# A11 of the first FFN step by products: loaded into the place of that step's own results

## The chip, the core and the metric

The kernel runs on one core of a Trainium2 chip. The core has a matrix engine (PE; its weight loads are listed as PEld), a vector engine (DVE), an activation engine (ACT), a general engine (POOL) and a queue engine (SP) that mostly issues DMA transfers. Each engine works through its own list of instructions in order; an instruction that waits holds up everything behind it on that engine. All transfers, whether SP, POOL or ACT issues them, are carried by the core's 16 DMA engines.

The metric is the device time of one execution in microseconds (us), given as the median of several runs.

## The reference

A two-layer network over 512 tokens of 1024 features: layer 0 mixes by dilated window attention, layer 1 by an mLSTM, and each is followed by a gated feed-forward part (FFN). The change lies in the first half of the FFN:

```python
def swiglu(xn, w_in, w_out):
    gu = xn @ w_in
    return (jax.nn.silu(gu[..., :D_FF]) * gu[..., D_FF:]) @ w_out
...
        h = h + swiglu(rms_norm(h, ffn_norm[i]), ffn_w_in[i], ffn_w_out[i])
```

with `D_FF` = 2816. All values are 32-bit floats.

## The kernel before

**Precision.** A product in full precision is made of three matmuls: each operand is split into a high part (rounded, made by ACT) and a low part (the rest, made by DVE), and high times high, high times low and low times high are added in PSUM (`SPLITS`). A weight tile of 128 x 1024 so costs ACT one copy (L209) and DVE one subtraction (L210) before PE can use it. The split weights live in three rotating buffers, the raw ones (`wraw`) in three as well.

**The FFN's first half** (`ffn_in`) runs over 22 blocks of 128 output columns, two at a time, j = 0, 2, ... 20. For j = 0 and 2 it works in the plain way (`plain`): PE multiplies weights by the split tokens, chunk by chunk, the result is scaled by the inverse norm (L982) and gated into a tile `hid` (L987). From j = 4 on (`PLAIN` = 4) it uses a scheme of seven products in place of eight (`PRODUCTS`): the weights of the two halves (gate and up) and of the two halves of the features form a 2 x 2 block A11, A12, A21, A22, the tokens a 2 x 2 block B11 to B22, and sums of both are multiplied.

- `normalized` makes the token operands once for each layer while the plain steps run on PE. It writes the normed tokens into two tiles, both of the rotating tag `w8` (two buffers): the first holds B11 and B12, the second B21 and B22. From these it makes T1 (L927), T3 (L932), T2 (L939) and T4 (L947), each in place or in the tile `t1`, and splits all of them (L909, L914). For B11 and T1 the low part is not a DVE subtraction: ACT writes minus the high part (L911) and a POOL transfer adds the raw values on the fly (L912).
- `weights_of(j)` loads the four weight tiles of a step (L1003, all on SP, in the order A11, A22, A12, A21). A11 and A21 lie in the two halves of a `w8` tile, that is, for j = 4 in the place of the first tokens' tile, for j = 6 in that of the second, and so on by turns; A22 and A12 lie in `wraw` buffers. `prepare` splits one operand after another, two products ahead of PE (`AHEAD`), and makes the sums (L1011): S1 = A21 + A22 and S2 = S1 - A11 in the tile `t1` (which T1 held), S3 = A11 - A21 in the place of A21, S4 = A12 - S2 in that of A12.
- `products(j)` issues the seven products in the order p1 (A11 B11), p5 (S1 T1), p6 (S2 T2), p2 (A12 B21), p7 (S3 T3), p3 (S4 B22), p4 (A22 T4), each 24 matmuls of 256 columns (L1040). The bank `u` starts as a copy of p1's result (L1052, ACT), takes p6, p7 and p4, and is read in between: after p7 by the addition into v5 (L1046, DVE). The results go into `hidden(j // 2)`: one half after p3 (L1079), one after p4 (L1083).

`hidden(i)` is a tile for each pair of blocks with its own tag and place; for i = 2, which belongs to j = 4, it is a tile of the FFN's own pool, `hid2`. Its space belongs to the mixer's tiles until the mixer is done, and is then not used until j = 4 writes its results.

Beside this, the first FFN (`output_products`) loads sums of output weight rows ahead of time: a plain load (L1161, SP) and a load that adds (L1162, POOL). The second FFN turns the residual: a DVE transpose (`hB`, L1690) and four stores on POOL (`hD`, L1693), and it loads and scales the final gains on POOL (L1711, L1712).

**What sets the order.** The program is written as above, but the framework's scheduler decides the order on each engine from estimated durations and dependences, for DMA issues on SP and POOL too. Tiles of one tag rotate: a new tile may be written when the last reader of the old one in the same bytes is done.

Of the kernel before, what the change touches and what calls it, by code (L numbers as in the profile page):

```python
# [71 lines left out]
def tile_hybrid_dilated_attn_mlstm(  # L72
# [131 lines left out]
    def split_chunk(chunk):  # L204

        raw, n, view, name = chunk
        hi = wp.tile([P, 1024], F32R, tag="whi", name=name + "_h", bufs=W_BUFS)
        lo = wp.tile([P, 1024], F32R, tag="wlo", name=name + "_l", bufs=W_BUFS)
        nc.scalar.activation(hi[:, :n], raw[:, :n], AF.Copy)  # L209
        nc.vector.tensor_tensor(lo[:, :n], raw[:, :n], hi[:, :n].bitcast(F32), op=ALU.subtract)  # L210
        return view(hi), view(lo)
# [147 lines left out]
    with ExitStack() as actx:  # L359
# [16 lines left out]
        ang, n, sn, cs = (tmp[:, 0, i * P:(i + 1) * P] for i in range(4))  # L376
# [497 lines left out]
    PLAIN = 4  # L874
    AHEAD = 2

    def ffn_in(layer, fp, pair, rbc, hook, following, hid, during):
# [11 lines left out]
        def place(i, name, dtype):  # L889
            p, tag = (xp, "x%d" % (i - 3)) if 3 <= i < 11 else (fp, "hid%d" % i)  # L890
            return p.tile([P, 2, SEQ], dtype, tag=tag, name="f%d%s%d" % (layer, name, i))

        def hidden(i):
            return place(i, "hid", F32)
# [98 lines left out]
        def weights_of(j):  # L993

            nm = "f%dj%d" % (layer, j)
            w8 = fp.tile([P, 2, 1024], F32, tag="w8", name=nm + "_w8", bufs=2)
            w = {"A11": w8[:, 0], "A21": w8[:, 1]}
            for key in ("A22", "A12"):
                w[key] = wp.tile([P, 1024], F32, tag="wraw", name=nm + key, bufs=W_BUFS)
            for key in ("A11", "A22", "A12", "A21"):  # L1000
                half, ch = int(key[1]) - 1, int(key[2]) - 1
                c0 = half * D_FF + j * P
                nc.sync.dma_start(w[key].rearrange("p (k n) -> p k n", k=4),  # L1003
                                  wi[ch * 4 * P:(ch + 1) * 4 * P, c0:c0 + 256].rearrange("(k p) n -> p k n", p=P))

            def split(key):
                return split_chunk((w[key], 1024, lambda t: t.rearrange("p (k n) -> p k n", k=4), nm + key))

            def total(key, a, b, op, place):
                w[key] = w[place]  # L1010
                nc.vector.tensor_tensor(w[key], w[a], w[b], op=op)  # L1011
            w["own"] = fp.tile([P, 1024], F32, tag="t1", name=nm + "S")
            made = {}

            def prepare(key):
                made[key] = split(key)

                if key == "A11":
                    total("S1", "A21", "A22", ALU.add, "own")
                elif key == "S1":  # L1020
                    total("S2", "S1", "A11", ALU.subtract, "own")
                elif key == "S2":
                    total("S3", "A11", "A21", ALU.subtract, "A21")
                elif key == "A12":
                    total("S4", "A12", "S2", ALU.subtract, "A12")
            return [(lambda key=key: prepare(key)) for key, _ in PRODUCTS], made
# [65 lines left out]
        def prepare(n):  # L1092
            if n < len(todo):
                j, i = todo[n]
                if j not in prepared:
                    prepared[j] = weights_of(j)
                prepared[j][0][i]()
            else:
                following(n - len(todo))
# [732 lines left out]
```

## Time and profile before

| | us |
|---|---|
| median of 3 runs | 1411.19 |
| range of the runs | 1411.02 to 1411.64 |
| the profiled execution | 1411.64 |
| its span, first to last instruction | 1409.9 |
| PE busy in the span | 1393.7 |
| DVE busy in the span | 1063.9 |

The profile is that of one execution. A row of a timeline gives the start (us from the span's start), the duration, engine, line, operation, output <- inputs with their sizes, and in brackets the idle time of the engine before it and what ended it. A row of a group ends with busy time, mean duration and idle time; a row of a tile's or line's view gives the count, the shortest, median and longest duration in ns, and the first and last start. A row of waits reads "who waited <- for whom: total us, times, longest". Names leave out buffer numbers, and a name that ends in one loses it: `f0j4A_h` is the high part of A11, A12 or A22 of layer 0's step j = 4, `f0j4S` one of its sums, `f0j_w` its `w8` tile, `f0x` a tile of normed tokens, `f0j_c`, `f0j_p` and `f0j_u` the banks c11, p5 and u. "DMA to landing" is the time from the issue of a transfer to its arrival.

### The profile page before, as it was taken

Reading aid. Unit: us, or ns where it says so; the run is one execution under the profiler, and the core shown is the slowest. Engines: PE = TensorE matmul, PEld = TensorE weight load, DVE = VectorE, ACT = ScalarE, POOL = GpSimd, SP = SyncE. Lnnn points to the kernel's source line nnn. Section 1 sums busy time; section 2 is a strip of 40 time slices with the busy share of each in tenths; the row PEclk is TensorE's granted clock in tenths of the full one; section 3 lists DMA queues with packets and bytes.
Section 4 is the critical chain, followed back from the end, with each engine's and each line's share of the span. In section 5 each row is a group of like instructions: output and inputs, shape, how many; then the busy total and the mean of one; then the engine's idle time right before and its main releaser. Section 6 shows DMA issues by size and latency. Waiting matters only on the chain. (4 is left out here: it accounts for less than half of the span.)

```text
span 1409.9 us, 21577 instructions
## 1 busy us (share of the span) xinstructions
PE 1393.7 (99%) x8370; PEld 1243.1 (88%) x8370; DVE 1063.9 (75%) x1838; ACT 677.8 (48%) x1127; POOL 153.5 (11%) x226
## 2 busy tenths in 40 slices
PE   9999999999999999999999999999999999999998
PEld 7888888888888888999999998888888899999886
DVE  7866557566567299877877898998758988887875
ACT  5333224224225254444576463786535544458744
POOL 1011011002002000000000101113101320001111
PEclk9999999999999999999999999999999999999999
DMA  6346245335434447333253733234334743335871
GB/s 194 96 114 196 82 118 160 119 106 131 159 105 121 155 145 175 115 120 114 83 171 83 162 109 105 81 87 105 101 98 116 213 123 121 120 107 118 174 193 60
DMA packets 138623, 178.15 MB, mean 126 GB/s; under 512 B 8660, under 2 KB 112404, under 8 KB 138520
## 3 DMA queue, kind: packets, MB, share of 16 engines
q1 hardware_dynamic: 121392, 134.17, 30.7%
q0 software_dynamic: 15472, 41.47, 13.4%
q8 instruction: 66, 1.08, 0.3%
q10 hardware_dynamic: 1656, 1.12, 0.2%
q14 instruction: 37, 0.30, 0.1%
HBM read 158.91 MB, written 15.73 MB: 124 GB/s over the span
## 5 line engine op out<-in xcount | busy, mean ns | idle before, releaser
L1162 POOL DMA_DIRECT2D f0S<-in_ffn_w_out_dram x10 | 8.7, 898 | 255.8 <-DVE f0hid L1079 173.6
L1187 POOL DMA_DIRECT2D f1T<-in_ffn_w_out_dram x12 | 14.3, 1189 | 197.2 <-ACT f1T L1190 169.8
L1693 POOL DMA_DIRECT2D hD<-hB x32 | 21.7, 695 | 70.2 <-DVE hB L1690 70.0
L552 DVE TENSOR_TENSOR rot<-rot,sinr 32x1024 f32<-32x1024 f32 x24 | 28.8, 1205 | 0.0
L240 PE MATMUL mo<-n_h,mo_k_h 128*128 128x512 f32 x64 | 25.3, 396 | 0.0
L240 PE MATMUL mo<-n_h,mo_k_l 128*128 128x512 f32 x64 | 25.2, 394 | 0.0
L240 PE MATMUL mwo<-yo_l,mwo_k_h 128*128 128x512 f32 x64 | 25.1, 393 | 0.0
L240 PE MATMUL mqk<-n_h,mqk_k_h 128*128 128x512 f32 x64 | 25.1, 392 | 0.0
L240 PE MATMUL mo<-n_l,mo_k_h 128*128 128x512 f32 x64 | 25.1, 392 | 0.0
L240 PE MATMUL awo<-ao_h,awo_k_h 128*128 128x512 f32 x64 | 25.1, 392 | 0.0
L240 PE MATMUL mqk<-n_l,mqk_k_h 128*128 128x512 f32 x64 | 25.1, 392 | 0.0
L240 PE MATMUL f0j<-n_h,f0j_h 128*128 128x512 f32 x64 | 25.0, 391 | 0.0
L240 PE MATMUL f1j<-n_h,f1j_h 128*128 128x512 f32 x64 | 25.0, 391 | 0.0
L240 PE MATMUL mwo<-yo_h,mwo_k_l 128*128 128x512 f32 x64 | 25.0, 391 | 0.0
L240 PE MATMUL mqk<-n_h,mqk_k_l 128*128 128x512 f32 x64 | 25.0, 391 | 0.0
L240 PE MATMUL awo<-ao_h,awo_k_l 128*128 128x512 f32 x64 | 25.0, 390 | 0.0
L240 PE MATMUL f1j<-n_h,f1j_l 128*128 128x512 f32 x64 | 25.0, 390 | 0.0
L240 PE MATMUL awo<-ao_l,awo_k_h 128*128 128x512 f32 x64 | 25.0, 390 | 0.0
L240 PE MATMUL f0j<-n_h,f0j_l 128*128 128x512 f32 x64 | 24.9, 390 | 0.0
L240 PE MATMUL f0j<-n_l,f0j_h 128*128 128x512 f32 x64 | 24.9, 389 | 0.0
L240 PE MATMUL f1j<-n_l,f1j_h 128*128 128x512 f32 x64 | 24.9, 389 | 0.0
L240 PE MATMUL mwo<-yo_h,mwo_k_h 128*128 128x512 f32 x64 | 24.8, 391 | 0.0
(2406 smaller groups left out, 5619.3 us busy)
## 6 DMA issues: line engine op xcount, KB each, us to landing
f0j_w<-in_ffn_w_in_dram SPq DMA_DIRECT2D x26, 512.0 KB, 4.9
f1j_w<-in_ffn_w_in_dram SPq DMA_DIRECT2D x26, 512.0 KB, 5.2
f1T<-in_ffn_w_out_dram POOLq DMA_DIRECT2D x12, 512.0 KB, 7.2
awo_k_w<-in_attn_w_out_dram SPq DMA_DIRECT2D x8, 512.0 KB, 7.0
mv_k_w<-in_mlstm_w_in_dram SPq DMA_DIRECT2D x8, 512.0 KB, 3.7
mqk_k_w<-in_mlstm_w_in_dram SPq DMA_DIRECT2D x8, 512.0 KB, 3.7
mo_k_w<-in_mlstm_w_in_dram SPq DMA_DIRECT2D x8, 512.0 KB, 4.1
mwo_k_w<-in_mlstm_w_out_dram SPq DMA_DIRECT2D x8, 512.0 KB, 3.5
```

The costliest lines, as they stand in the source:

```text
L240: nc.tensor.matmul(acc, whl[a][:, k, m * P:(m + 1) * P], pairs[b][kk], start=(kk == 0 and (a, b) == SPLITS[0]), stop=(kk == nk - 1 and (a, ...
L552: nc.vector.tensor_tensor(sh, sh, sinr.unsqueeze(1).to_broadcast([R, 2, SEQ]), op=ALU.mult)
L1162: nc.gpsimd.dma_start(t, src[1][:, ks], accum_op=ALU.add)
L1187: nc.gpsimd.dma_start(view(to), weight_rows(hk * UNITS + u, n), accum_op=ALU.add)
L1693: nc.gpsimd.dma_start(hD[k // 4].rearrange("(b i) x -> i b x", i=R)[:, :, c0:c0 + R], t[R * a_:R * (a_ + 1)])
```

## The change

For j = 4 alone, A11 is loaded into a tile from `hidden(2)`, the place that later takes the results of the same step, and not into the first half of the `w8` tile. A21 stays where it was.

```diff
             w8 = fp.tile([P, 2, 1024], F32, tag="w8", name=nm + "_w8", bufs=2)
-            w = {"A11": w8[:, 0], "A21": w8[:, 1]}
+
+            a11 = hidden(j // 2).rearrange("p k n -> p (k n)") if j == PLAIN else w8[:, 0]
+            w = {"A11": a11, "A21": w8[:, 1]}
             for key in ("A22", "A12"):
```

The step's own `hidden(2)` call in p3 then takes the same tag a second time; all readers of A11 (its split and the sums S2 and S3) stand ahead of p3 on their engines. The number and kinds of instructions are the same; the line numbers behind the edit grow by two. In the built program the scheduler's order differs around the start of j = 4 in both layers: the load of A11 stands further ahead on SP, and on DVE the split of A11 and the sums stand further ahead, T4 and its split further back; in layer 1 residual transposes and the loading of the final gains also change places.

## The prediction

> **What bounds the kernel now.** I read the page first, then who waits for whom on PE, then the starts of PE's products.
>
> ```profile
> span 1409.9 us, 21577 instructions
> PE 1393.7 (99%) x8370; PEld 1243.1 (88%) x8370; DVE 1063.9 (75%) x1838; ACT 677.8 (48%) x1127; POOL 153.5 (11%) x226
> ```
>
> PE is busy for 99% of the span, so only a place where it stops can give time. Three of its longer waits lie in the step the change touches:
>
> ```profile
> PE f1j_p L1040 <- DVE f1j4S_l L210: 1.3, 1, 1.3
> ...
> PE f0j_u L1040 <- ACT f0j_u L1052: 1.1, 1, 1.1
> ...
> PE f0j_u L1040 <- DVE f0j4S_l L210: 0.7, 1, 0.7
> ```
>
> The ends of matmuls are modelled, so the loss is better read from starts. The first product of a step, A11 times B11, begins (last numbers: first and last start) at:
>
> ```profile
> L1040 PE MATMUL f0j_c<-f0B11h,f0j4A_h x8: 277/283/284, 549.0 to 551.5; 128*128 128x256 f32 x8
> L1040 PE MATMUL f0j_c<-f0B11h,f0j6A_h x8: 282/283/284, 571.6 to 574.1; 128*128 128x256 f32 x8
> L1040 PE MATMUL f0j_c<-f0B11h,f0j8A_h x8: 283/283/284, 591.7 to 594.2; 128*128 128x256 f32 x8
> L1040 PE MATMUL f1j_c<-f1B11h,f1j4A_h x8: 278/283/284, 1109.1 to 1111.6; 128*128 128x256 f32 x8
> L1040 PE MATMUL f1j_c<-f1B11h,f1j6A_h x8: 283/284/284, 1132.3 to 1134.8; 128*128 128x256 f32 x8
> ```
>
> Step j=6 lasts 591.7 - 571.6 = 20.1 us: seven products of 2.87 us, without a gap. Step j=4 lasts 22.6 in layer 0 and 23.2 in layer 1. The excess, 2.5 + 3.1 = **5.6 us**, is all that the change can win in these steps. In the first of them DVE, not PE, is the full engine:
>
> ```profile
> 548.95:571.60 22.65, 20.83 (x170) 20.35 (x169) 21.20 (x24) 10.74 (x13) 2.60 (x3) 1.00 0.76 209
> ```
>
> (length; PE, PEld, DVE, ACT, POOL busy; clock; DMA share; GB/s). DVE is full because it stood still just before (timeline of DVE, and one row of ACT):
>
> ```profile
> 536.47 1.22 DVE L914 TENSOR_TENSOR f0T3l<-f0x,f0T3h 128x1024 fp32r<-128x1024 f32 x1
> ...
> 541.70 1.22 DVE L947 TENSOR_TENSOR f0x<-f0x 128x1024 f32<-128x1024 f32 x1
> ...
> 545.11 1.06 ACT L209 ACTIVATE f0j4A_h<-f0j_w 128x1024 fp32r<-128x1024 f32 x1 [5.19 <-DMA f0j_w<-in_ffn_w_in_dram]
> ...
> 546.21 1.23 DVE L210 TENSOR_TENSOR f0j4A_l<-f0j_w,f0j4A_h 128x1024 fp32r<-128x1024 f32 x1 [3.29 <-ACT f0j4A_h L209]
> ...
> 547.95 1.22 DVE L1011 TENSOR_TENSOR f0j4S<-f0j_w,f0j4A 128x1024 f32<-128x1024 f32 x1
> 549.08 1.22 DVE L914 TENSOR_TENSOR f0T4l<-f0x,f0T4h 128x1024 fp32r<-128x1024 f32 x1
> 550.22 0.69 DVE L982 TENSOR_TENSOR f0j2gu<-f0j,n1rbc 128x512 f32<-128x512 f32 x1
> ...
> 561.16 1.22 DVE L1011 TENSOR_TENSOR f0j6S<-f0j_w,f0j6A 128x1024 f32<-128x1024 f32 x1
> ...
> 566.00 0.69 DVE L1046 TENSOR_TENSOR f0j4v<-f0j_u,f0j4v 128x512 f32<-128x512 f32 x1 [0.20 <-PE f0j_u L1040]
> ```
>
> T3's low part (536.47) is the last reader of the first tokens' tile; only then may A11 be fetched into it. It lands at 545.1, DVE idles 3.29 us for its split, and S1 = A21 + A22 starts at 547.95.
>
> **The change part by part.** *Removed:* A11's wait for the tokens. Its load goes, in the built order, to a place long ahead: behind the first plain weight load of layer 0 and before the last load of the mLSTM's output weights in layer 1. In layer 0 it waits there for the last attention matmul that reads the space of `hid2`. There the DMA engines are idle:
>
> ```profile
> 485.00:490.00 5.00, 5.00 (x24) 4.14 (x23) 0.09 (x1) 0.00 (x0) 0.00 (x0) 1.00 0.00 0
> ```
>
> The next load on SP needs a weight buffer that is still in use, so I cost the early load at nothing. Were it held longer, the plain weights behind it would be late, and PE would pay each us in full.
>
> *Not removed:* A21 still goes into the tokens' tile, after T3, and S1 also overwrites T1, which the accumulating transfer of T1's low part must have read. So S1 moves up only as far as these two land sooner:
>
> ```profile
> L912 POOL DMA_DIRECT2D f0T1l<-f0t x1: 877/877/877, 537.6 to 537.6; - x1
> ...
> DMA to landing us min/median/max: 7.7/7.7/7.7
> ```
>
> ```profile
> q1 hardware_dynamic: 1556, 1.55, 59.3%
> q0 software_dynamic: 144, 0.52, 36.3%
> ```
>
> ```profile
> 546.00:548.00 2.00, 2.00 (x10) 1.68 (x9) 1.79 (x3) 1.64 (x3) 0.00 (x0) 1.00 0.00 1
> ```
>
> From 538 to 546 SP's three weight loads took 59.3% of 8 us, 1.6 us each; T1's transfer landed at 545.3, and all was quiet by 546 (A21 landed near 545.8). Without A11 the same work ends 1.6 us sooner: S1 can start at 544.3. Bounds: 543.3 if A21 and T1 share well, 545.1 if A21 gets no more than A11's old place.
>
> Layer 1, in the same way:
>
> ```profile
> L1003 SPq DMA_DIRECT2D f1j_w<-in_ffn_w_in_dram x2: 368/918/1467, 1099.5 to 1099.9; - x2
> ...
> DMA to landing us min/median/max: 7.8/7.8/7.8
> ```
>
> ```profile
> 1106.10 1.06 ACT L209 ACTIVATE f1j4A_h<-f1j_w 128x1024 fp32r<-128x1024 f32 x1 [3.59 <-DMA f1j_w<-in_ffn_w_in_dram]
> ```
>
> ```profile
> 1101.00:1103.00 2.00, 2.00 (x11) 1.65 (x9) 1.97 (x4) 1.24 (x2) 1.58 (x3) 1.00 1.05 131
> ```
>
> A11 landed at 1106.1, A21 at 1107.7. A11's 1.6 us leaves, and so do the four 64 KB stores of a residual block, whose transpose the new order puts behind A12's split: at the 131 GB/s of their window up to 2 us, of which I take 1.7. S1 at 1104.4; bounds 1103.3 and 1106.1.
>
> The Trainium skill (DMA: Bandwidth & Descriptors, Queues, rings and completion order) says that on each DMA engine the descriptors of one queue are consumed in ring order. By that A21 just takes A11's place: S1 at 545.1 and 1106.1, the first rival below. Layer 1 agrees (A21 1.6 us behind A11), layer 0 does not (0.7).
>
> *The gaps.* With S1 at 544.3, the low part of S1 is ready 4.0 us later and that of S2 8.1 us later (long DVE instructions every 1.135 us, 549.08 less 547.95; short ones 0.6, since 547.95 - 546.21 = 1.74 holds one of each): 548.3 and 552.4. PE wants them at 551.8 and 554.7. In layer 1: 1108.4 and 1112.5 against 1112.0 and 1114.8. All 5.6 us of gaps go, even at the late bounds.
>
> *Moved:* T4 (L947 and its split), which filled DVE's idle time, now stands behind S2's low part. From S1's start to the end of T4's low part the new order has 8 long and 6 short DVE instructions: 8 x 1.135 + 6 x 0.6 = 12.7 us, so 557.0 instead of 550.3. That end frees the second tokens' tile for **A11 and A21 of j=6**, now issued 6.7 us later, at 557.1 and 557.5. DVE's S1 of j=6 waits for the second of them, and behind it in DVE's queue stand A22's low part, S3 of j=6 and the v5 addition (L1046), which must read bank u before product seven, A22 times T4, may add to it. So p4 pays. Pairs of such loads took:
>
> ```profile
> L1003 SPq DMA_DIRECT2D f0j_w<-in_ffn_w_in_dram x2: 368/437/506, 550.3 to 550.7; - x2
> ...
> DMA to landing us min/median/max: 3.8/4.3/4.9
> ```
>
> ```profile
> L1003 SPq DMA_DIRECT2D f0j_w<-in_ffn_w_in_dram x2: 379/512/644, 561.3 to 561.7; - x2
> ...
> DMA to landing us min/median/max: 4.9/5.5/6.0
> ```
>
> ```profile
> L1003 SPq DMA_DIRECT2D f1j_w<-in_ffn_w_in_dram x2: 367/438/508, 1116.6 to 1117.0; - x2
> ...
> DMA to landing us min/median/max: 4.1/4.7/5.2
> ```
>
> Layer 0 meets the accumulating loads of the output weights as the second pair did, but partly: 5.4, between 4.9 and 6.0. Landing 557.5 + 5.4 = 562.9; then 3 x 1.135 + 0.69 + 0.1 = 4.2: v5 is done at 567.1. PE wants p4 at 549.0 + 6 x 2.87 = 566.2: **0.9 us lost**. Layer 1: in the new order POOL scales the final gains here and not at
>
> ```profile
> 1137.77 2.47 POOL L1712 TENSOR_SCALAR gbc<-gbc 128x512 f32<-128x512 f32 x1
> ```
>
> ```profile
> 1138.91 1.51 DVE L1011 TENSOR_TENSOR f1j8S<-f1j_w,f1j8A 128x1024 f32<-128x1024 f32 x1
> ```
>
> where a 1.22 us addition took 1.51, so +0.3: T4 ends at 1104.4 + 12.7 + 0.3 = 1117.4, the second load goes at 1117.9, lands 5.2 later at 1123.1, v5 ends at 1127.3; p4 is wanted at 1126.3: **1.0 lost**. After each stop PE's first matmuls come slower, 0.1 each. In step j=6 DVE has 3.8 us to spare, so the delay ends there:
>
> ```profile
> 571.60:591.70 20.10, 20.10 (x169) 20.10 (x169) 16.34 (x17) 9.88 (x12) 0.00 (x0) 1.00 0.35 106
> ```
>
> Sum: -5.6 + 0.9 + 1.0 + 0.2 = **-3.5 us**. The profiled execution took 1411.64 (span 1409.9 and 1.7 around it), so 1408.1; it is 0.45 above the median of 1411.19, so 1407.7.
>
> **The rivals.** *A21 no earlier than A11's old place* (S1 at 545.1 and 1106.1): 0.8 and 1.7 us are added to the new waits, 1.7 + 2.7 + 0.2 = 4.6 against 5.6, time 1410.2. For it: A21's own wait is untouched. Against it: less is in flight.
>
> *No new wait*: S1 at 543.3 and 1103.3, and second loads after 4.9 and 5.2 us: v5 ends at 565.6 and 1126.2, before p4. All 5.6 us stay: 1405.6. Against it: both have to be at their best.
>
> *Slower:* the second step's weights become the bound. If S1 is at the late bounds and those loads take the 7.8 us of layer 1's A21, v5 ends at 570.3 and 1131.6: 4.1 + 5.3 + 0.2 = 9.6 against 5.6, 1415.2. It decides above 5.6 us of new waits; with S1 as forecast, only when both second loads take about 7 us or more. For it: T4 is moved whole behind S2. Against it: the three pairs shown took at most 6.0.
>
> *It doesn't do what it says:* A11's split still starts late (its weight buffers wait for a plain chunk on PE, two chunks before the end): no change, 1411.2. DVE was held by the DMA and not by that, so it is unlikely.
>
> **How the numbers follow.** Forecast 0.47, no new wait 0.17, A21 in the old place 0.24, slower 0.07, nothing gained 0.05. What counts as different is 0.2%, 2.8 us: the first two are faster (0.64), the third and the last the same (0.29). The range, 1405.5 to 1410.3, runs from no new wait to A21 in the old place; the slower case and the last are left out.
>
> **What would show it.** A11's split on ACT near 538 and no 3.29 us idle on DVE; S1 near 544.3 and 1104.4; no wait of PE on S1 or S2; T4's low part ending near 557 and 1117.4; j=6's S1 on DVE waiting for a DMA; one wait of PE of about 1 us on v5 (L1048 in the new numbering) in each layer; step lengths of 21.1 us, step j=6 still 20.1. The forecast is wrong if PE stops in a plain step, or if p4 waits for more than 2 us.

## The result and the profile after

The changed kernel takes **1415.35 us** (median of 7 runs, 1414.08 to 1418.76) beside 1411.02 for the kernel before (1410.65 to 1412.55): a ratio of 1.0033, with a 95% interval of 1.0021 to 1.0045. It is slower by 4.3 us, above the forecast range of 1405.5 to 1410.3, and close to the 1415.2 of the rival "slower".

The profiled execution took 1414.08 us; it is the fastest of the seven, 1.3 us below their median. Its page begins:

```profile
span 1412.3 us, 21568 instructions
...
PE 1393.4 (99%) x8370; PEld 1243.2 (88%) x8370; DVE 1063.1 (75%) x1838; ACT 677.9 (48%) x1127; POOL 152.4 (11%) x226
```

PE is as busy as before (1393.7): the 2.4 us of span are not work. The first product of each step begins (the view of the tile B11's high part, one row for each step; last numbers: first and last start):

```profile
L1042 PE MATMUL f0j_c<-f0B11h,f0j4A_h x8: 278/283/283, 547.8 to 550.3; 128*128 128x256 f32 x8
...
L1042 PE MATMUL f0j_c<-f0B11h,f0j6A_h x8: 280/284/287, 575.0 to 577.5; 128*128 128x256 f32 x8
...
L1042 PE MATMUL f0j_c<-f0B11h,f0j8A_h x8: 280/283/287, 595.2 to 597.7; 128*128 128x256 f32 x8
```

```profile
L1042 PE MATMUL f1j_c<-f1B11h,f1j4A_h x8: 277/283/283, 1112.6 to 1115.1; 128*128 128x256 f32 x8
...
L1042 PE MATMUL f1j_c<-f1B11h,f1j6A_h x8: 283/283/283, 1134.7 to 1137.2; 128*128 128x256 f32 x8
```

Step j=4 now lasts 575.0 - 547.8 = **27.2 us in layer 0**, 4.6 more than before, and 22.1 in layer 1, 1.1 less. The next step is 20.2, as ever. The difference of the two, 3.5 us, less the 1.2 us by which this execution reached step j=4 earlier (547.8 for 549.0), leaves 2.3 of the 2.4 us of span. The waits of PE say what fills the 27.2:

```profile
PE f0j_u L1042 <- DVE f0j4v L1048: 4.5, 1, 4.5
PE f1j_u L1042 <- DVE f1j4v L1048: 1.3, 1, 1.3
...
PE f0j_u L1042 <- ACT f0j4u L1064: 0.6, 1, 0.6
```

Every wait of before on S1 or S2 in these steps is gone. In their place PE waits on v5 ahead of p4, 4.5 us in layer 0. DVE's timeline shows why v5 is late:

```profile
544.37 1.22 DVE L1013 TENSOR_TENSOR f0j4S<-f0j_w,f0j4A 128x1024 f32<-128x1024 f32 x1 [2.66 <-DMA f0T1l<-f0t]
...
556.00 1.22 DVE L914 TENSOR_TENSOR f0T4l<-f0x,f0T4h 128x1024 fp32r<-128x1024 f32 x1
...
566.33 1.23 DVE L1013 TENSOR_TENSOR f0j6S<-f0j_w,f0j6A 128x1024 f32<-128x1024 f32 x1 [5.54 <-DMA f0j_w<-in_ffn_w_in_dram]
...
569.74 0.68 DVE L1048 TENSOR_TENSOR f0j4v<-f0j_u,f0j4v 128x512 f32<-128x512 f32 x1
```

S1 of j=4 starts at 544.37 and T4's low part ends at 557.2, as the change's new order has it. Three more instructions follow, and then DVE stands idle for 5.54 us until the second weight load of j=6 has landed. That load's own view (one row for the pair; the landing is that of the second):

```profile
L1005 SPq DMA_DIRECT2D f0j_w<-in_ffn_w_in_dram x2: 379/522/664, 557.2 to 557.7; - x2
...
DMA to landing us min/median/max: 8.6/8.6/8.6
```

The pair is issued right behind T4, at 557.2 and 557.7, and the second takes **8.6 us**. And there is a second loss, in the table by stretches (length; PE, PEld, DVE, ACT, POOL busy with counts; granted clock; DMA share; GB/s):

```profile
565.80:570.60 4.80, 0.31 (x4) 0.14 (x2) 4.28 (x5) 1.22 (x2) 0.00 (x0) 1.00 0.84 262
570.60:571.00 0.40, 0.40 (x3) 0.40 (x4) 0.40 (x1) 0.00 (x0) 0.00 (x0) 1.00 1.00 335
571.00:574.40 3.40, 3.40 (x19) 3.40 (x17) 3.40 (x5) 0.63 (x1) 0.00 (x0) 0.50 0.24 78
574.60:575.00 0.40, 0.40 (x5) 0.40 (x5) 0.40 (x1) 0.00 (x0) 0.00 (x0) 1.00 0.00 0
```

In the 4.8 us to 570.6 PE is busy for 0.31, the modelled ends of what came before, and from 571.0 to 574.4 its clock is granted at 0.50: 19 matmuls in 3.4 us, where 0.4 us at full clock hold 5. p4 so takes 575.0 - 570.57 = 4.4 us instead of 2.87.

### The profile page after: what moved, and what is told of

It reads as the page before. It is cut to its first block, busy times and chain, and to the rows that moved or that the text cites. A ratio compares the mean times of both kernels' runs of the same rounds, so it can differ in the third digit from the quotient of the medians.

```text
span 1412.3 us, 21568 instructions
## 1 busy us (share of the span) xinstructions
PE 1393.4 (99%) x8370; PEld 1243.2 (88%) x8370; DVE 1063.1 (75%) x1838; ACT 677.9 (48%) x1127; POOL 152.4 (11%) x226
```

## The experiments

Every experiment ran beside the kernel before. Lengths of step j=4 are those of the profiled execution, layer 0 and layer 1.

| kernel | median us (range) | ratio to before, 95% interval | step j=4 |
|---|---|---|---|
| before | medians of 1411.02 to 1411.96 in the four sets | | 22.6, 23.2 |
| the change | 1415.35 (1414.08 to 1418.76) | 1.0033, 1.0021 to 1.0045 | 27.2, 22.1 |
| the change again | 1415.46 (1411.62 to 1417.52) | 1.0025, 1.0016 to 1.0033 | 27.9, 22.2 |
| layer 0 only | 1415.14 (1413.78 to 1416.30) | 1.0021, 1.0012 to 1.0030 | 26.5, 23.3 |
| layer 1 only | 1411.59 (1410.49 to 1413.75) | 0.9997, 0.9988 to 1.0006 | 24.0, 22.6 |
| no adding transfers | 1410.86 (1409.11 to 1411.99) | 0.9989, 0.9980 to 0.9998 | 21.4, 22.5 |
| PE filled, half a bank | 1412.79 (1411.72 to 1414.29) | 1.0007, 0.9999 to 1.0016 | 24.6, 22.1 |
| PE filled, whole bank | 1412.66 (1411.34 to 1415.15) | 1.0009, 1.0000 to 1.0018 | 25.6, 24.4 |
| S1 in a place of its own | 1414.35 (1413.25 to 1415.73) | 1.0020, 1.0011 to 1.0029 | 27.0, 22.0 |
| j=6 elsewhere | 1409.87 (1409.05 to 1411.93) | 0.9986, 0.9977 to 0.9994 | 21.0, 23.3 |
| T4 first | **1406.15** (1405.64 to 1406.65) | 0.9955, 0.9942 to 0.9967 | 20.2, 20.2 |
| before, T4 first | 1412.55 (1412.29 to 1413.38) | 1.0005, 0.9996 to 1.0015 | 23.7, 23.1 |

**One layer at a time.** The condition gets `and layer == 0`, or `and layer == 1`:

```diff
-            a11 = hidden(j // 2).rearrange("p k n -> p (k n)") if j == PLAIN else w8[:, 0]
+            a11 = hidden(j // 2).rearrange("p k n -> p (k n)") if j == PLAIN and layer == 0 else w8[:, 0]
```

> The change in layer 0 alone; layer 1 as before. Theory (the second step's weights come late in layer 0, PE stops 4.5 us ahead of p4 there and then runs 3.7 us at half clock): the whole loss is here. Step j=4 of layer 0 about 27 us, step j=4 of layer 1 23.2 as before, time about 4.6 us above before: 1415.6. Rival (the loss lies in layer 1, or is spread over the program by the moved loads): layer 0 alone costs nothing or gains its 2.5 us, 1408.5 to 1411.

> The change in layer 1 alone; layer 0 as before. Theory: step j=4 of layer 1 lasts 22.1 us where it lasted 23.2, one wait of 1.3 us ahead of p4, time 1.1 us below before: 1409.9. Rival (the loss lies in layer 1 or elsewhere): 1412 or more.

Layer 0 alone brings the loss: 3.2 us, with a step of 26.5 and a wait of 3.7 us on v5. Layer 1 alone is 0.4 us below before, with an interval that holds 1: its gain of 0.6 to 1.1 us in the step is too small to be told in the time, and 1409.9 was missed. (In its profiled execution layer 0, which is as before there, took 24.0 us; the last section comes back to that.)

**T4 ahead of the weights.** Three steps of `normalized` are issued ahead of the first weights, not one:

```diff
-        some(1)
+        some(3)
         for n in range(AHEAD):
```

> The change, with T2, B21 and T4 written ahead of the first weights of j=4, so that T4's subtraction and its low part stand around S1 on DVE and no longer behind the low part of S2; the two first weights of j=6 then stand ahead of the output weight rows in SP's order. Theory (T4 late is the cause): they are issued near 547.5 in layer 0, 10 us sooner than after the change, and land near 553; PE does not stop ahead of p4, its clock stays 1.00; S2's low part is the one that may now come late, up to 0.8 us. Steps j=4 of 20.1 to 21 us in both layers, time 4 to 5.5 us below before: 1405.6 to 1407. Rival (the loss comes from the early A11, or from the accumulating transfers alone): the stop ahead of p4 stays over 2 us, time above 1411.

It came, and with 5.8 us the gain is even a little above the 4 to 5.5 of the theory. The pair for j=6 is issued near 548, ahead of the output rows, and nobody waits for it:

```profile
L1005 SPq DMA_DIRECT2D f0j_w<-in_ffn_w_in_dram x2: 368/434/500, 547.9 to 548.3; - x2
...
DMA to landing us min/median/max: 4.3/4.8/5.4
```

```profile
L1042 PE MATMUL f0j_c<-f0B11h,f0j4A_h x8: 277/283/283, 549.3 to 551.9; 128*128 128x256 f32 x8
...
L1042 PE MATMUL f0j_c<-f0B11h,f0j6A_h x8: 283/283/283, 569.5 to 572.0; 128*128 128x256 f32 x8
```

```profile
L1042 PE MATMUL f1j_c<-f1B11h,f1j4A_h x8: 278/283/283, 1107.1 to 1109.6; 128*128 128x256 f32 x8
...
L1042 PE MATMUL f1j_c<-f1B11h,f1j6A_h x8: 283/283/283, 1127.3 to 1129.8; 128*128 128x256 f32 x8
```

Both steps last 20.2 us, which is a step without a gap, and the kernel is 5.8 us faster than before and 9 us faster than the change: the 5.6 us of gaps, whole. S2's low part came in time. T4's place is what decides.

**T4 first without the change.** The same edit in the kernel before:

> The kernel before (A11 in the tokens' place) with T2, B21 and T4 written ahead of the first weights of j=4. Theory (the gain of the third run needs both: an early A11 for the gaps, and T4 ahead so that nothing new waits): A11 still lands late, PE's waits on S1 and S2 stay, steps j=4 of 22.5 to 24 us, time within 1 us of before. Rival (the order of T4 alone brings the gain): step j=4 near 20.2 us, time near 1406.

Nothing is gained (steps 23.7 and 23.1; the median is 1.1 us above that of before in its set, and the interval holds 1), since A11 still lands late. The early A11 opens the gain, and T4's place decides whether it is kept.

**The weights of j=6 in other places**, with T4 left late:

```diff
+            spare = lambda i: hidden(i).rearrange("p k n -> p (k n)")
+            if j == PLAIN + 2:
+                w = {"A11": spare(3), "A21": spare(4)}
```

> The change, and A11 and A21 of j=6 loaded into two free result tiles (those of j=6 and j=8) in place of the second tokens' tile; T4 stays where the change put it. Theory (what hurts is only that j=6's weights wait for T4's tile): DVE's S1 of j=6 finds its weights there, no stop ahead of p4, steps j=4 near 20.1 us in both layers, time 5 us below before: 1406. If the two loads, now early, crowd A21 of j=4, S1 of j=4 comes up to 2 us later and 1 us of that is paid. Rival (T4's own late place on DVE makes p4 wait, since DVE is full there): the stop ahead of p4 stays at 2 us or more even with the weights landed, time 1410 or more.

In layer 0 the theory holds: 21.0 us with T4 as late as in the change, and no wait on v5. So T4 hurts there through the loads that wait for its tile. Of the 0.9 us above a step without a gap, 0.6 is a wait of PE ahead of p7 for ACT's copy of u (L1066). The change has the same wait (the 0.6 in its list above), where the later wait on v5 hides it; whether it comes from T4's place was not tested. In layer 1 the two loads, now early, went out ahead of A21 of j=4, the crowding named in the expectation, and cost more than the 1 us allowed. DVE's S1 there, and the issue of A21:

```profile
1106.65 1.23 DVE L1015 TENSOR_TENSOR f1j4S<-f1j_w,f1j4A 128x1024 f32<-128x1024 f32 x1 [3.61 <-DMA f1j_w<-in_ffn_w_in_dram]
```

```profile
L1007 SPq DMA_DIRECT2D f1j_w<-in_ffn_w_in_dram x1: 368/368/368, 1097.3 to 1097.3; - x1
```

A21 went at 1097.3 and landed 9.2 us later; S1 starts 0.35 us ahead of p1 (1107.0), where the change has 3.8, and step j=4 is 23.3 us, no better than before. The time, 1409.87, so missed the 1406 of the theory.

**Why 8.6 us.** Without the three transfers that add output rows:

```diff
-                nc.gpsimd.dma_start(t, src[1][:, ks], accum_op=ALU.add)
+                if u != 3 and (u, ks.start) != (1, 0):
+                    nc.gpsimd.dma_start(t, src[1][:, ks], accum_op=ALU.add)
```

> The change, without the three transfers that add output weight rows (two parts of sum 3, one of sum 1) while j=6's first weights are on their way in layer 0; sums 1 and 3 then hold only the first of their two rows there. Everything else, T4's late place too, stays. Theory (the second load took 8.6 us and not 5.4 because these transfers ran beside it): it lands in about 5 us, near 562.8, v5 ends near 567, PE waits 1 to 1.5 us ahead of p4 instead of 4.5, too short for the clock to fall; step j=4 of layer 0 about 22 us instead of 27.2, time about 1410, which is what the prediction's sum would have given with its own terms. Rival (the load is slow because of the weight loads right behind it on the same queue, or because of the plain loads of the rows): it still takes 8 us or more, stop over 3.5 us, time above 1413.

```profile
L1005 SPq DMA_DIRECT2D f0j_w<-in_ffn_w_in_dram x2: 378/438/499, 557.6 to 558.0; - x2
...
DMA to landing us min/median/max: 4.7/4.7/4.7
```

```profile
PE f0j_u L1042 <- DVE f0j4v L1048: 0.6, 1, 0.6
```

The load that took 8.6 us takes 4.7, with T4 just as late (the pair goes at 557.6 and 558.0) and the same plain loads around it. The wait on v5 is 0.6 us, and layer 0's step 21.4. The queues of the two kernels between 556 and 568 us (packets, MB, share of the 16 engines' time), the change and then this one:

```profile
q1 hardware_dynamic: 2284, 2.28, 58.4%
q0 software_dynamic: 422, 0.77, 41.9%
```

```profile
q1 hardware_dynamic: 3067, 3.05, 78.9%
```

The adding transfers (q0) moved 0.77 MB in 41.9% of 12 us, 153 GB/s for the time they held the engines; the plain loads (q1) 2.28 MB in 58.4%, 325 GB/s, about the same as without them (3.05 MB in 78.9%: 322). Two stretches of the kernel before tell whether it is the adding or the queue that POOL feeds. In the first, 1295 to 1303 us, only transfers that add run (L1187); in the second, 1109 to 1114 us, only plain loads that POOL issues (L1705 and L1711):

```profile
q0 software_dynamic: 599, 1.16, 99.1%
```

```profile
q0 software_dynamic: 302, 1.00, 61.5%
```

That is 146 GB/s for the transfers that add, with nothing beside them, and 325 GB/s for the plain ones. So the adding transfers hold the engines twice as long for each byte, with plain loads beside them and without, and that time the weights lack. The Trainium skill (DMA: Bandwidth & Descriptors, SWDGE vs HWDGE vs iDMA) says that an engine takes its hardware-fed and its software-fed queues by turns. The shares of 58.4% and 41.9% do not speak against that, but no run here shows the turns themselves.

**Is the half clock from standing still?** Spare matmuls on PE between p3 and p4 of layer 0, the wait on v5 left in place. The first form writes only half of a bank, and some of the kernel's values change with it; the second form, further below, leaves them as they are. (Where the expectations speak of 3.7 us at half clock, the table above has 3.4.)

```diff
             def p4():
+                if layer == 0 and j == PLAIN:
+                    b = ops["B11"][0]
+                    spare = ps.tile([P, 512], F32, tag="t", name=nm + "idle", bufs=1)
+                    for _ in range(34):
+                        nc.tensor.matmul(spare[:, :HALF], b[:, 0, :P], b[:, 0], start=True, stop=True)
```

> The change, with 34 spare matmuls of 256 columns (about 4.1 us, into a bank that nobody reads) on PE between p3 and p4 of j=4 in layer 0: the wait on v5 stays, but PE is busy during it. Theory (the clock falls to a half because PE stood idle, and stays there 3.7 us): granted clock 1.00 throughout 565 to 580, p4 again 2.9 us long, step j=4 about 25.5 us instead of 27.2, time about 1.7 us below the change's 1415.35, that is 1413.6, and a smaller spread from run to run. Rival (the clock falls for another reason, such as the load on the DMA engines): p4 still takes 4.4 us or more, time 1415 or above.

The second form writes the whole bank, with `spare` and `b[:, 0:2]` as one row of 512 columns, 18 times. The change ran once more beside it:

> The changed kernel once more, as a yardstick beside the next two. Theory (the length of the stop ahead of p4 and, on top of it, one or two stretches of 3.4 us at half clock change from run to run): 1414 to 1419 again, its runs spread over some 4 us; step j=4 of layer 0 26 us or more, with a stop of 3.5 us or more. Rival (the earlier runs were a chance): 1412 or less.

> The change, with 18 spare matmuls of 512 columns (about 4.1 us) over a whole bank between p3 and p4 of j=4 in layer 0. Theory (the clock falls because PE stands idle): granted clock 1.00 from 565 to 580, p4 2.9 us long, step j=4 24.5 to 25.5 us, time 1.7 to 3 us below the changed kernel beside it, and its runs closer together. Rival: the clock falls here too, p4 takes 4.4 us or more, and the time is that of the changed kernel.

The stretches of the whole-bank form around the stop, in layer 0 and, in the last two rows, in layer 1:

```profile
565.00:575.00 10.00, 9.60 (x64) 8.56 (x64) 8.31 (x9) 2.75 (x3) 0.00 (x0) 1.00 0.59 189
1128.90:1131.80 2.90, 0.82 (x7) 0.65 (x6) 2.90 (x4) 1.06 (x1) 0.00 (x0) 0.98 1.08 351
1132.00:1135.20 3.20, 3.20 (x18) 3.20 (x16) 3.20 (x6) 0.63 (x1) 1.35 (x3) 0.51 0.39 107
```

In layer 0 the clock stays at 1.00 although v5 is as late as ever (p4 goes at 570.9 and takes 3.0 us), and the two forms have medians 2.6 and 2.8 us below those of the change and of its repeat. (In the first form's profile the landing took only 7.2 us, so its gain is not the clock's alone.) So it is the standing still, and not the load on the DMA engines, that halves the clock there. The mean granted clocks of all runs say the same: 0.995 to 0.997 in all seven of the change, 0.998 or 0.999 in all eleven of the first form and in ten of the eleven of the second. The runs of the second form did not come closer together (1411.34 to 1415.15): in the profiled one, at 1415.15 the slowest of them, the clock fell in layer 1 instead, behind a wait of only 2.1 us. The spread itself of the change (1414 to 1419, and 1411.6 to 1417.5 when repeated) is so not explained by layer 0 alone. It goes with the clock, though: the one run of the repeat with a mean clock of 0.999 took 1411.62, the nine with 0.996 or 0.997 took 1413.2 to 1417.5. The profile of the repeat, at 1415.71, has a landing of 9.3 us, a stop of 5.2 and 6.8 us at half clock.

**What S1 waited for.** S1 and S2 of j=4 in a free tile, not in T1's:

```diff
-            w["own"] = fp.tile([P, 1024], F32, tag="t1", name=nm + "S")
+            w["own"] = (hidden(3).rearrange("p k n -> p (k n)") if j == PLAIN else
+                        fp.tile([P, 1024], F32, tag="t1", name=nm + "S"))
```

> The change, and S1 and S2 of j=4 written into a free result tile instead of T1's tile, so that S1 no longer waits for the adding transfer of T1's low part (7.9 us, landed 3.4 us ahead of p1 in the changed kernel). Theory (in layer 0 this transfer and not A21 is what S1 waited for, and it did not get faster when A11's load left): S1 of j=4 starts when A21 has landed, 1 us or more sooner than 3.4 us ahead of p1, T4's low part and j=6's loads follow by up to 1 us, and the stop ahead of p4 shortens by as much: time up to 2.5 us below the changed kernel. Layer 1 as in the changed kernel (S1 waits for A21 there). Rival (A21 lands no sooner than T1's transfer): S1 of j=4 still starts about 3.4 us ahead of p1, nothing changes.

S1 now waits for A21, and starts at:

```profile
543.82 1.23 DVE L1013 TENSOR_TENSOR f0hid<-f0j_w,f0j4A 128x1024 f32<-128x1024 f32 x1 [1.95 <-DMA f0j_w<-in_ffn_w_in_dram]
```

That is 4.2 us ahead of p1 (548.0) instead of 3.4. The theory has the releaser right, but the gain is 0.8 us, not 1 or more. The pair of j=6 still took 8.5 us, the stop was 4.4, and the intervals of this kernel and of the change's repeat overlap: for the time it is inconclusive.

## Why the prediction was wrong, point by point

**Right:** the old gaps. All 5.6 us of them went, and T4 first shows that they were worth just that. Right, too, was the new chain: T4 moved behind S2's low part, the second tokens' tile and with it j=6's pair late, DVE held at S1 of j=6, v5 behind it, p4 behind v5. Even its tail fits: from landing (566.3) to v5's end (570.4) 4.1 us for a forecast of 4.2. In layer 1 (DVE, then the pair's load):

```profile
1108.80 1.23 DVE L1013 TENSOR_TENSOR f1j4S<-f1j_w,f1j4A 128x1024 f32<-128x1024 f32 x1 [1.93 <-DMA f1j_w<-in_ffn_w_in_dram]
...
1120.45 1.19 DVE L914 TENSOR_TENSOR f1T4l<-f1x,f1T4h 128x1024 fp32r<-128x1024 f32 x1
```

```profile
L1005 SPq DMA_DIRECT2D f1j_w<-in_ffn_w_in_dram x2: 367/440/512, 1121.7 to 1122.1; - x2
...
DMA to landing us min/median/max: 4.3/4.8/5.3
```

From S1 to T4's end 12.8 us for 13.0, and the second load in 5.3 us for 5.2.

**The step that failed** is the price of the landing in layer 0: "Layer 0 meets the accumulating loads of the output weights as the second pair did, but partly: 5.4, between 4.9 and 6.0". It was 8.6, and 7.2 to 9.3 in the five other profiles with that order and those transfers. The adding transfers as POOL issues them, in the kernel before and in the changed one:

```profile
L1162 POOL DMA_DIRECT2D f0S<-in_ffn_w_out_dram x3: 852/858/1207, 556.8 to 558.6; - x3
```

```profile
L1164 POOL DMA_DIRECT2D f0S<-in_ffn_w_out_dram x3: 851/856/969, 554.2 to 556.6; - x3
```

The pairs of before that gave the price went at 550.3, 6.5 us ahead of these transfers, and at 561.3, when the last of them was 2.7 us on its way. The change put the pair at 557.2, with all three issued in the 3 us ahead of it. The order of SP shows why: before, the pair went at 550.3 and the plain loads of the output rows from 553.3 on; in the changed kernel the rows go from 550.8 on and the pair behind them. The prediction took A11's new place from the built order, but not this. Without those transfers the load takes 4.7 us and the step 21.4, for the 21.1 forecast. That these two are so near is partly luck: from p1 the second load goes 0.9 us later there than forecast and lands 0.7 sooner. And that kernel is only 0.6 us below before in its set, not 3.5, in part because its layer 1 takes 22.5 and not 21.1.

**Two smaller terms** failed with it. "Without A11 the same work ends 1.6 us sooner: S1 can start at 544.3" was 4.7 us ahead of p1 and came to 3.4 in layer 0, outside the bounds, since S1 waits there for T1's adding transfer (the releaser in its row above), which took as long without A11 beside it as with it (7.7):

```profile
L912 POOL DMA_DIRECT2D f0T1l<-f0t x1: 877/877/877, 536.4 to 536.4; - x1
...
DMA to landing us min/median/max: 7.9/7.9/7.9
```

In layer 1 it came to 3.8: A21 took 5.8 us there, 2.0 less than before, where the prediction took off 3.3 for A11 and the four stores. And "After each stop PE's first matmuls come slower, 0.1 each" was 1.5 us after the long stop. The Trainium skill (TensorE: Matmul & The Clock Gate, Part 1: The HAM clock gate) has PE's clock halved after an idle window of about 3.4 us until one such window has been busy. The trace agrees with the half and with 3.4 us as the length of the slow stretch; on what brings it on, the last section has more. It did not enter the sum because the stop was forecast at 0.9.

Layer 0, from p1: the second load goes 1.4 us later than forecast (9.9 for 8.5), takes 3.2 longer, and v5 ends 4.5 later. The forecast excess of 1.0 becomes 1.0 + 4.5 + 1.5 = 7.0, measured 27.2 - 20.1 = 7.1. Layer 1: S1's 0.9 us are all that is missing, 2.0 for 1.1 (its p1 was at 1112.6). New losses of 9.1 stand against 5.6 us of gaps.

**The rivals.** "Slower: the second step's weights become the bound" had the mechanism, the decision point (5.6 us of new waits) and nearly the time, with a chance of 0.07. What spoke against it, that "the three pairs shown took at most 6.0", was no evidence for a pair in another neighbourhood. That its time is so near is partly luck: it had 4.1 and 5.3 us of new waits in the two layers, and measured are 7.1 and 2.0. It named S1 at its late bounds as a condition as well; the landing in layer 0 and the clock were enough. "A21 no earlier than A11's old place": A21 landed 4.2 us ahead of p1 in layer 0 (S1 in a place of its own) and 3.8 in layer 1, between the forecast (4.7 in both) and this rival (3.9 and 3.0). It decided nothing. The sign given for a wrong forecast, a wait of over 2 us ahead of p4, is the one that appeared.

## What to carry to other kernels

Taking away a wait lets the scheduler reorder what used to fill it; follow each displaced instruction to the tile that it frees and to the transfer that waits for that tile. Price that transfer among the neighbours that it will have in the new order, not by its length in the old one. And an early operand pays only when the release of the next one's place stays early too: here one line that keeps T4 ahead turns 4.3 us of loss into 5.8 of gain.

## What the runs showed of the hardware

**The clock falls by fixed stretches, and after short stops too.** In the twelve profiles there are six such stretches away from the kernel's last microseconds, three of 3.4 us and three of 6.8. With the change the half clock lasted 3.4 us (571.0 to 574.4) and began 0.4 us behind the stop of 4.5. With layer 0 alone it lasted twice that, and began 2.4 us into a stop of 3.7 (565.6 to 569.3):

```profile
568.00:574.80 6.80, 5.51 (x26) 5.54 (x27) 5.76 (x8) 0.81 (x2) 0.00 (x0) 0.50 0.28 89
574.80:575.20 0.40, 0.40 (x5) 0.40 (x5) 0.40 (x1) 0.40 (x1) 0.00 (x0) 0.99 0.00 0
```

With layer 1 alone it fell in layer 0, whose order is that of before, with no long stop at all:

```profile
553.60:557.20 3.60, 1.84 (x14) 1.48 (x13) 3.60 (x5) 3.54 (x5) 1.64 (x2) 1.00 0.65 213
557.40:560.60 3.20, 3.20 (x17) 3.20 (x16) 3.20 (x4) 0.68 (x1) 0.78 (x1) 0.50 0.94 144
560.80:562.00 1.20, 1.20 (x12) 1.20 (x12) 1.20 (x2) 0.67 (x2) 0.00 (x0) 1.00 1.07 206
```

PE was busy for 1.84 of the 3.6 us ahead of it, with two waits of 1.0 and 0.7 us. The old gaps so cost a further 1.4 us in that execution (step of 24.0 for 22.6), which fits the spread of the kernel before (1410.5 to 1413.9 in its runs): of its 81 runs beside the experiments, the 40 with a mean clock of 0.999 took 1411.4 us on average and the four with 0.996 or 0.997 took 1413.6, though no profile of it shows the fall. The Trainium skill (TensorE: Matmul & The Clock Gate, Part 1: The HAM clock gate) speaks of an idle window; here a stretch in which PE was busy for half the time stood ahead of a fall. It does not always bring one. The kernel before has nearly the same waits in its profile (1.1 and 0.7 us), and its clock stayed:

```profile
554.80:558.40 3.60, 1.78 (x13) 1.40 (x12) 3.60 (x5) 3.60 (x5) 1.58 (x2) 1.00 0.69 228
558.40:562.00 3.60, 3.60 (x32) 3.60 (x32) 3.60 (x4) 1.55 (x3) 1.02 (x2) 1.00 0.93 144
```

A stop of 2.1 us was followed by a fall in the whole-bank form, one of 2.3 us in "before, T4 first" was not. What share of which stretch decides was not settled.

**An adding transfer is twice as dear to the engines as its bytes say** (146 and 153 GB/s beside 322 to 325 for plain loads, on SP's queue and on POOL's), and what it delays is the plain load next to it: 8.6 us for 4.7.
